# Hybrid decoder block on one core: the row norm of x from its natural layout, spread over the partitions by ones times a diagonal

## Chip, cores and metric

One core of one Trainium2 chip runs the whole program in a single launch. The metric is the device time of that launch in microseconds; lower is better.

## The reference, cut to what matters

The block starts with an RMS norm of `x` (1024 rows of 1024 values), and every projection reads its result:

```python
def rms_norm(x, w):
    xf = x.astype(jnp.float32)
    y = xf * lax.rsqrt(jnp.mean(xf * xf, axis=-1, keepdims=True) + EPS)
    return (y * w.astype(jnp.float32)).astype(x.dtype)

h = rms_norm(x, norm_w)
proj = h @ w_in          # split into the inputs of three mixers and the merge gates
...
x = x + merged @ w_out
```

After it come three mixers (a spatial gate, windowed attention, cross attention into `mem`), three projections under sigmoid gates, and an output projection with the residual add. The change touches only how the root mean square of each row of `x` is found and applied.

## The kernel before, in words

Every fp32 matmul of the large projections is made of three passes: each operand is split into a high part (a rounded cast by ScalarE, `A.copy`, L137) and a low part (the difference, by VectorE, L138), and `mm3` (L158) multiplies high by high, high by low and low by high. So weights and activations all pass through ScalarE and VectorE before TensorE uses them.

The host gives `x` twice: `xT`, transposed and cut into five column groups (columns are rows of x), and `x` in its natural layout (until now read only near the end, for the residual add). The groups are `x0` (rows 0 to 127), `x1` (rows 512 to 639), then `x2`, `x3`, `x4`, each of 256 columns: rows 128 a to 128 a + 127 and the same plus 512, for a = 1, 2, 3.

The prologue, L288 to L328, works through the groups. `load_x` (L231) starts the transfers of a group's pages from SyncE's queue (512 KB each, eight in all). `square_x` and `squares` (L237, L175) square a group on ScalarE into tiles of the ring `ws` (four buffers of 128x512 in `wpool`); for x3 and x4 VectorE first adds the tiles in pairs (L189). `sum_x` and `sum_squares` (L242, L193) multiply an all-ones matrix with the squares on TensorE, which sums over the partitions and leaves each column's sum in all 128 partitions of a PSUM bank (ring `tr`, two banks). `norm_x` and `normalize` (L245, L199) take the root on ScalarE (L203) and the reciprocal on VectorE (L204) over the whole 128 x width tile `rsx`, multiply `xT` by the norm weight and by `rsx` (VectorE, L208, eight instructions a group) and split the result. `sums` (L261) makes differences of normalized quarters for a fast matrix multiplication later. `proj_mq(j)` (L275) is the first projection: for each block of 128 rows j, in the order 0, 4, 1, 5, 2, 6, 3, 7, 24 matmuls of 128x512 with eight weight pieces `wq_[k]`. Blocks 0 and 4 need x0 and x1, blocks 1 and 5 need x2, 2 and 6 x3, 3 and 7 x4. The argument `between` puts a `sum_x` in the midst of a projection. After it come the `n` products (L968 on), whose first weights `wh_n`, `wl_n` are made while the projections end.

Three things set the order. The program is traced in the order of the lines, and a scheduler at compile time places each engine's instructions by that priority and by what it believes to be ready; at run time every engine's queue is in order. The eight pieces of `w_mq` (`raw`, L140) come through the same ring `ws` as the squares: a piece can only be transferred once the buffer's earlier user is done. And `rsx` lies in the ring `wl`, nine buffers, beside the weights' low parts.

Of the kernel before, what the change touches and what calls it, by code (L numbers as in the profile page):

```python
# [12 lines left out]
F32 = mybir.dt.float32  # L13
F32R = mybir.dt.float32r
I32 = mybir.dt.int32
AF = mybir.ActivationFunctionType
# [5 lines left out]
P = 128  # L22
D = 1024
# [18 lines left out]
def hybrid_block(  # L42
# [131 lines left out]

    def squares(xs, cw, name, eng, levels=1):  # L175

        kp = KT // len(xs)
        kq = 512 // cw
        sqs = []
        for k in range(0, KT, kq):  # L180
            sq = wpool.tile([P, kq, cw], F32, name=f"xq_{name}{k}", tag="ws", bufs=4)
            last[0] = A.activation(out=sq, in_=xs[k // kp][:, k % kp:k % kp + kq, :], func=AF.Square)
            sqs.append(sq)
        for _ in range(levels):
            h = len(sqs) // 2
            if h == 0:
                break
            for i in range(h):
                eng.tensor_tensor(out=sqs[i], in0=sqs[i], in1=sqs[h + i], op=ALU.add)  # L189
            sqs = sqs[:h]  # L190
        return [sq[:, k, :] for sq in sqs for k in range(kq)]

    def sum_squares(sqs, cw, name):  # L193
        pt = ps.tile([P, 512], F32, name=f"np_{name}", tag="tr")[:, :cw]
        for k, sq in enumerate(sqs):
            T.matmul(pt, lhsT=ones, rhs=sq, start=k == 0, stop=k == len(sqs) - 1)
        return pt

    def normalize(xs, pt, wcol, dst, cw, name, rs):  # L199


        kp = KT // len(xs)
        A.activation(out=rs, in_=pt, func=AF.Sqrt, scale=1.0 / D, bias=eps_c)  # L203
        V.reciprocal(out=rs, in_=rs)  # L204
        for k0 in range(0, KT, 4):
            xp, q = xs[k0 // kp], k0 % kp
            for k in range(4):
                V.scalar_tensor_tensor(out=xp[:, q + k, :], in0=xp[:, q + k, :], scalar=wcol[:, k0 + k:k0 + k + 1],  # L208
                                       in1=rs, op0=ALU.mult, op1=ALU.mult)
            for hi, lo, xv in dst(k0, xp[:, q:q + 4, :]):  # L210
                split(hi, lo, xv)
# [19 lines left out]
    def load_x(i):  # L231
        o = sum(widths[:i]) * KT
        xcs.append(load_cols(xT[:, o:o + widths[i] * KT], widths[i], f"x{i}"))

    sq_ = {}

    def square_x(i):  # L237
        sq_[i] = squares(xcs[i], widths[i], f"x{i}", V, int(i > 2))

    sm_ = {}  # L240

    def sum_x(i):  # L242
        sm_[i] = sum_squares(sq_[i], widths[i], f"x{i}")

    def norm_x(i):  # L245
        def dst(k0, xv):
# [7 lines left out]
            if k0 == 0:  # L254
# [3 lines left out]
                    + (xv.rearrange("p k (b t) -> p k b t", b=2),)]  # L258
        normalize(xcs[i], sm_[i], nw, dst, widths[i], f"x{i}", rs=rsx[:, 256 * (i % 2):256 * (i % 2) + widths[i]])

# [27 lines left out]
    rsx = wpool.tile([P, WW], F32, name="rsx", tag="wl", bufs=9)  # L288
    load_x(0)
    load_consts()  # L290
    wraw = [raw(w_mq[:, k * 512:(k + 1) * 512], 512, f"mq{k}") for k in range(2)]
    load_x(1)
    square_x(0)
    sum_x(0)
    with tc.issue_after(last[0].ins):
        wq_ = [parts(wraw[k], 512, f"mq{k}") for k in range(2)]
    norm_x(0)
    for k in range(2, 4):
        wq_.append(parts(raw(w_mq[:, k * 512:(k + 1) * 512], 512, f"mq{k}"), 512, f"mq{k}"))
    square_x(1)  # L300
    sum_x(1)
# [711 lines left out]
    with tc.tile_pool(name="ppool", reuse_waits="tile", bufs=1, side="right") as pp_:  # L1013
# [41 lines left out]
        def mem_norm(c):  # L1055
            cs = slice(c * P, (c + 1) * P)
            normalize([xm[c]], sm[c], mw,
                      lambda k0, xv: [(mem[0][:, k0:k0 + 4, cs], mem[1][:, k0:k0 + 4, cs], xv)], P, f"mem{c}", page([P, 256], f"rs_mem{c}", tag="th")[:, :P])

# [457 lines left out]
```

## Time and profile before

| | |
|---|---|
| median of 3 runs | 1120.58 us (1119.02 to 1123.42) |
| the profiled execution's own time | 1120.26 us |
| its span, first to last instruction | 1118.5 us |
| TensorE busy | 1092.7 us, 98% |
| VectorE busy | 794.1 us, 71% |
| ScalarE busy | 514.0 us, 46% |
| mean granted TensorE clock | 0.994 of full speed |

The profile is one execution. A busy share is a mean over the whole span: it says which engine carries the kernel, and the stretches of the prologue have to be looked at by themselves. The three runs differ by 0.4%.

### The profile page before, as it was taken

The numbers are of one execution on the slowest core, as the hardware profiler recorded it, in microseconds if no ns is written. First come the engines' busy times: TensorE is split into PE (matmuls) and PEld (weight loads), VectorE is DVE, ScalarE is ACT, GpSimd is POOL, SyncE is SP. The second block draws the span as 40 slices with busy tenths as digits, with TensorE's granted clock in tenths as the row PEclk, the third lists the DMA queues.
The fourth block names the chain that finished last, engine by engine and source line by source line (L and its number), as shares of the span: only waits on it lengthen the run. The fifth ranks groups of instructions, "written<-read, shape, count | busy, mean of one in ns | idle before, by whom it ended". The sixth has DMA issues, their size and how long they took to land.

```text
span 1118.5 us, 18302 instructions
## 1 busy us (share of the span) xinstructions
PE 1092.7 (98%) x6680; PEld 955.9 (85%) x6680; DVE 794.1 (71%) x1701; ACT 514.0 (46%) x1123; POOL 195.7 (17%) x250
## 2 busy tenths in 40 slices
PE   8989999999999999999999999999999999998998
PEld 7879999999988887888888888888888787886998
DVE  6999899856687766656555656687885467568863
ACT  6553333223245543755665554666564562134320
POOL 0000431321000002011111111111111026511232
PEclk9999999999999999999999999999999999999999
DMA  7222322454242423444434325455544975665432
GB/s 236 76 96 91 128 86 96 144 190 151 72 142 94 129 98 119 143 147 153 128 121 136 124 95 181 123 180 157 166 132 132 335 273 160 173 161 136 142 107 83
DMA packets 84558, 157.57 MB, mean 141 GB/s; under 512 B 9605, under 2 KB 30708, under 8 KB 84468
## 3 DMA queue, kind: packets, MB, share of 16 engines
q1 hardware_dynamic: 68164, 106.87, 30.6%
q0 software_dynamic: 14864, 47.05, 13.0%
q10 hardware_dynamic: 1440, 2.49, 0.6%
q8 instruction: 52, 0.85, 0.3%
q14 instruction: 38, 0.31, 0.1%
HBM read 106.84 MB, written 48.22 MB: 139 GB/s over the span
## 4 chain that ended last, share of the span: by engine, by line
PE 86%; DVE 5%; DMA 4%; issue 3%; POOL 1%; ACT 1%; SPq 0%; POOLq 0%; DVEq 0%; ACTq 0%
PE t L159 12%; PE t L161 12%; PE t L160 11%; PE n L160 7%; PE n L159 7%; PE n L161 7%; PE po L606 3%; PE pp L159 2%; DMA merged<-tg 2%; PE pp L161 2%; PE pp L160 2%; PE po L160 2%; PE po L159 2%; PE po L161 2%; PE pt L599 1%
## 5 line engine op out<-in xcount | busy, mean ns | idle before, releaser
L159 PE MATMUL t<-th,wh_t 128*128 128x512 f32 x336 | 135.2, 402 | 0.0
L161 PE MATMUL t<-th,wl_t 128*128 128x512 f32 x336 | 132.0, 393 | 0.0
L160 PE MATMUL t<-tl,wh_t 128*128 128x512 f32 x336 | 131.4, 391 | 0.0
L159 PE MATMUL n<-wh_n,th 128*128 128x256 f32 x384 | 108.2, 282 | 0.0
L161 PE MATMUL n<-wh_n,tl 128*128 128x256 f32 x384 | 107.6, 280 | 0.0
L160 PE MATMUL n<-wl_n,th 128*128 128x256 f32 x384 | 107.6, 280 | 0.0
L161 PEld LDWEIGHTS t<-th,wl_t 128*128 128x128 f32 x336 | 63.1, 188 | 14.5
L159 PEld LDWEIGHTS n<-wh_n,th 128*128 128x128 f32 x384 | 73.3, 191 | 1.5 <-issue 0.9
L160 PEld LDWEIGHTS t<-tl,wh_t 128*128 128x128 f32 x336 | 63.3, 188 | 12.8
L159 PEld LDWEIGHTS t<-th,wh_t 128*128 128x128 f32 x336 | 63.3, 188 | 12.3
L160 PEld LDWEIGHTS n<-wl_n,th 128*128 128x128 f32 x384 | 72.1, 188 | 0.2 <-issue 0.2
L161 PEld LDWEIGHTS n<-wh_n,tl 128*128 128x128 f32 x384 | 72.2, 188 | 0.0
L159 PE MATMUL t<-H2h,wh_t 128*128 128x512 f32 x168 | 67.8, 404 | 0.0
L137 ACT CAST wh_t<-ws_t 128x512 fp32r<-128x512 f32 x86 | 51.8, 619 | 33.3 <-PE n L161 11.8
L161 PE MATMUL t<-H2h,wl_t 128*128 128x512 f32 x168 | 65.9, 392 | 0.0
L160 PE MATMUL t<-H2l,wh_t 128*128 128x512 f32 x168 | 65.5, 390 | 0.0
L138 DVE TENSOR_TENSOR wl_t<-ws_t,wh_t 128x512 fp32r<-128x512 f32 x86 | 58.2, 685 | 10.0 <-ACT wh_t L137 9.9
L1069 DVE TENSOR_TENSOR o<-t,sa 128x512 f32<-128x512 f32 x63 | 43.3, 687 | 29.5 <-PE t L161 25.1
L1038 POOL DMA_DIRECT2D scr_g<-o x48 | 26.1, 544 | 191.9 <-ACT o L1024 167.1
L939 POOL TENSOR_TENSOR on<-on,nss 128x1024 f32<-128x1024 f32 x12 | 26.2, 2205 | 173.4 <-DVE nss L134 116.0
L159 PE MATMUL n<-wh_n,H2h 128*128 128x256 f32 x192 | 54.9, 286 | 0.1
L160 PE MATMUL n<-wl_n,H2h 128*128 128x256 f32 x192 | 54.3, 283 | 0.0
(382 smaller groups left out, 3185.1 us busy)
## 6 DMA issues: line engine op xcount, KB each, us to landing
ws_t<-in_w_t SPq DMA_DIRECT2D x64, 256.0 KB, 3.5
scr_g<-o POOLq DMA_DIRECT2D x48, 256.0 KB, 2.7
tg<-scr_g SPq DMA_DIRECT2D x16, 512.0 KB, 3.9
ws_n<-in_w_n SPq DMA_DIRECT2D x24, 256.0 KB, 3.3
wr_n<-in_w_n SPq DMA_DIRECT2D x24, 256.0 KB, 3.3
scr_qk<-on POOLq DMA_DIRECT2D x12, 512.0 KB, 4.3
bx<-scr_qk SPq DMA_DIRECT2D x24, 256.0 KB, 3.3
wr_t<-in_w_t SPq DMA_DIRECT2D x20, 256.0 KB, 3.5
```

The lines of the kernel that those rows point to most:

```text
L137: A.copy(out=hi, in_=y)
L138: (eng or V).tensor_tensor(out=lo, in0=y, in1=hi.bitcast(F32), op=ALU.subtract)
L159: T.matmul(o, lhsT=ah, rhs=bh, start=first, stop=False)
L160: T.matmul(o, lhsT=ah, rhs=bl, start=False, stop=False)
L161: T.matmul(o, lhsT=al, rhs=bh, start=False, stop=last)
L599: T.transpose(p2[:, h * P:(h + 1) * P], c.pr[h // 2][:, h % 2, b * P:(b + 1) * P], ident)
L606: T.matmul(po[:, 64 * h:64 * h + 64], lhsT=c.pT[b][:, h * P:(h + 1) * P], rhs=mb.v[:, (t - nk + 1 + b) % 3, 64 * h:64 * h + 64], start=b = ...
L939: G.tensor_tensor(out=v, in0=v, in1=ss[:, 16 * ORD[q]:16 * ORD[q] + 16].unsqueeze(2) .to_broadcast([P, 16, 64]), op=ALU.mult)
L1038: G.dma_start(out=t[:, h], in_=d)
L1069: V.tensor_tensor(out=o[q], in0=psum, in1=s, op=ALU.add)
```

## The change

The sums of squares of x are no longer made from `xT`. For each block t of 128 rows, `square_x` now loads the natural rows of `x` in two halves of 128x512 (16 transfers of 256 KB in all, from SyncE's queue, into the ring `ws`), and ScalarE squares each half with an accumulator output, which leaves the row sums in one column of `ssq`. VectorE adds the two halves, ScalarE takes the root and VectorE the reciprocal, each on a 128x1 column. `sum_x` then multiplies the identity by that column (VectorE, 128x128, into a quarter of `rsx`) and TensorE multiplies ones with that diagonal: 1/rms of the block's rows stands in all partitions of a PSUM bank. `normalize` reads it from PSUM as its second tensor operand. `square_x(0)` stands ahead of the constants and the first weights, and `square_x(1)` behind `norm_x(0)`, ahead of weight pieces 2 and 3. `square_x(2)`, `(3)`, `(4)` stay where they were. The norm of `mem` keeps its way: its root and reciprocal are written out in `mem_norm`.

```diff
-    def squares(xs, cw, name, eng, levels=1):
...
-            last[0] = A.activation(out=sq, in_=xs[k // kp][:, k % kp:k % kp + kq, :], func=AF.Square)
...
-                eng.tensor_tensor(out=sqs[i], in0=sqs[i], in1=sqs[h + i], op=ALU.add)
...
-    def normalize(xs, pt, wcol, dst, cw, name, rs):
+    def normalize(xs, rs, wcol, dst):
...
-        A.activation(out=rs, in_=pt, func=AF.Sqrt, scale=1.0 / D, bias=eps_c)
-        V.reciprocal(out=rs, in_=rs)
...
-    sq_ = {}
+    GROUPS = ((0,), (4,), (1, 5), (2, 6), (3, 7))
+    ssq = const.tile([P, 32], F32, name="ssq")
+    rst = const.tile([P, 16], F32, name="rst")
 
     def square_x(i):
-        sq_[i] = squares(xcs[i], widths[i], f"x{i}", V, int(i > 2))
+        for t in GROUPS[i]:
+            for h in range(2):
+                xn = wpool.tile([P, WW], F32, name=f"xn{t}{h}", tag="ws", bufs=4)
+                nc.sync.dma_start(out=xn, in_=x[t * P:(t + 1) * P, 512 * h:512 * h + 512])
+                last[0] = A.activation(out=xn, in_=xn, func=AF.Square, accum_out=ssq[:, 2 * t + h:2 * t + h + 1])
+            r = rst[:, 2 * t:2 * t + 1]
+            V.tensor_tensor(out=r, in0=ssq[:, 2 * t:2 * t + 1], in1=ssq[:, 2 * t + 1:2 * t + 2], op=ALU.add)
+            A.activation(out=r, in_=r, func=AF.Sqrt, scale=1.0 / D, bias=eps_c)
+            V.reciprocal(out=rst[:, 2 * t + 1:2 * t + 2], in_=r)
...
     def sum_x(i):
-        sm_[i] = sum_squares(sq_[i], widths[i], f"x{i}")
+        pt = ps.tile([P, 512], F32, name=f"rs_x{i}", tag="tr")
+        for n, t in enumerate(GROUPS[i]):
+            dg = rsx[:, (t % 4) * P:(t % 4 + 1) * P]
+            V.tensor_scalar(out=dg, in0=ident, scalar1=rst[:, 2 * t + 1:2 * t + 2], scalar2=None, op0=ALU.mult)
+            T.matmul(pt[:, n * P:(n + 1) * P], lhsT=ones, rhs=dg, start=True, stop=True)
+        sm_[i] = pt[:, :widths[i]]
...
     load_x(0)
+    square_x(0)
     load_consts()
     wraw = [raw(w_mq[:, k * 512:(k + 1) * 512], 512, f"mq{k}") for k in range(2)]
     load_x(1)
-    square_x(0)
     sum_x(0)
     with tc.issue_after(last[0].ins):
         wq_ = [parts(wraw[k], 512, f"mq{k}") for k in range(2)]
     norm_x(0)
+    square_x(1)
     for k in range(2, 4):
         wq_.append(parts(raw(w_mq[:, k * 512:(k + 1) * 512], 512, f"mq{k}"), 512, f"mq{k}"))
-    square_x(1)
     sum_x(1)
```

## Rows read from the trace of the kernel before

**Rows 1.** The page's part 1: busy time, share and instructions of each engine.

```profile
PE 1092.7 (98%) x6680; PEld 955.9 (85%) x6680; DVE 794.1 (71%) x1701; ACT 514.0 (46%) x1123; POOL 195.7 (17%) x250
```

**Rows 2.** Stretches of the prologue: length, busy time by engine, clock, DMA share, GB/s.

```profile
9.50:14.50 5.00, 2.05 (x16) 1.86 (x16) 4.04 (x11) 2.66 (x6) 0.00 (x0) 1.00 0.84 287
...
18.00:23.00 5.00, 4.82 (x21) 3.80 (x21) 4.70 (x13) 4.27 (x8) 0.00 (x0) 1.00 0.97 340
23.00:30.00 7.00, 7.00 (x32) 5.67 (x32) 7.00 (x13) 5.73 (x12) 0.00 (x0) 1.00 0.22 83
...
55.00:70.00 15.00, 12.71 (x55) 9.64 (x53) 15.00 (x28) 9.82 (x18) 0.00 (x0) 1.00 0.09 35
70.00:100.00 30.00, 28.98 (x240) 28.41 (x239) 26.80 (x46) 11.52 (x22) 0.00 (x0) 1.00 0.40 134
```

**Rows 3.** Timeline of TensorE: start, length, what, idle before and releaser.

```profile
10.65 2.05 PE L196 MATMUL np_x<-xq_x,ones 128*128 128x128 f32 x16 [1.21 <-ACT xq_x L182]
...
30.19 0.39 PE L159 MATMUL pq<-wh_mq,H1h 128*128 128x512 f32 x1
...
57.87 0.50 PE L159 MATMUL pq<-wh_mq,H1h 128*128 128x512 f32 x1 [2.01 <-ACT H1h L137]
...
69.65 0.40 PE L159 MATMUL n<-wh_n,H1h 128*128 128x256 f32 x2
```

**Rows 4.** Chain that ended last, prologue: start, length, what.

```profile
8.94 4.37 DMA ws_mq<-in_w_mq
...
19.74 3.68 PE np_x L196 x16
...
32.39 1.78 PE np_x L196 x8
...
46.99 1.73 PE np_x L196 x8
...
53.38 1.67 DVE rsx L204
...
72.61 0.61 DVE wl_n L138
```

**Rows 5.** Groups of VectorE by shape, first 75 us: busy, mean ns, idle before.

```profile
L208 DVE SCALAR_TENSOR_TENSOR xs_x<-xs_x,colt,rsx 128x256 f32<-128x256 f32 x24 | 9.8, 485 | 0.0
...
L204 DVE RECIPROCAL rsx<-rsx 128x256 f32<-128x256 f32 x3 | 5.3, 1752 | 0.0
L208 DVE SCALAR_TENSOR_TENSOR xs_x<-xs_x,colt,rsx 128x128 f32<-128x128 f32 x16 | 4.4, 347 | 0.0
...
L189 DVE TENSOR_TENSOR xq_x<-xq_x,xq_x 128x512 f32<-128x512 f32 x4 | 2.6, 699 | 0.0
...
L204 DVE RECIPROCAL rsx<-rsx 128x128 f32<-128x128 f32 x2 | 1.9, 950 | 0.0
```

**Rows 6.** Groups by shape, whole span: the nearest prices for the new operations.

```profile
L95 DVE TENSOR_SCALAR gb<-gb 128x24 f32<-128x24 f32 x1 | 0.2, 178 | 0.0
L733 DVE RECIPROCAL st_m<-st_m 128x2 f32<-128x2 f32 x16 | 2.6, 165 | 8.5 <-ACT pr_m L730 8.5
L911 DVE SCALAR_TENSOR_TENSOR off<-prs,colt,bsb 128x128 f32<-128x128 f32 x4 | 1.4, 347 | 0.0
L182 ACT ACTIVATE xq_x<-xs_x 128x512 f32<-128x512 f32 x16 | 9.3, 621 | 2.8 <-DMA xs_x<-in_xT 2.4 <-PE np_x L196 0.2
L591 ACT ACTIVATION_READ_ACCUMULATOR pr<-pr,ng 128x1 f32 x96 | 18.1, 188 | 0.0
L83 ACT ACTIVATE warm<-eps_c 128x1 f32<-128x1 f32 x1 | 0.2, 203 | 0.0
```

**Rows 7.** Transfers of the first 30 us: totals.

```profile
DMA packets 2786, 6.61 MB, mean 220 GB/s; under 512 B 608, under 2 KB 608, under 8 KB 2784
```

**Rows 8.** TensorE's clock around an idle stretch near the end (columns of rows 2).

```profile
1026.00:1028.00 2.00, 0.92 (x4) 0.95 (x5) 1.97 (x4) 0.63 (x1) 0.77 (x1) 0.73 0.39 106
1028.00:1030.00 2.00, 2.00 (x12) 2.00 (x11) 1.97 (x4) 0.32 (x1) 0.08 (x1) 0.50 0.90 180
```

More of the change, by code (lines that the diff above doesn't have):

```diff
@@ L173, in hybrid_block @@
     last = [None]
-    def squares(xs, cw, name, eng, levels=1):
[L177 to L181, printed above, removed]
-            last[0] = A.activation(out=sq, in_=xs[k // kp][:, k % kp:k % kp + kq, :], func=AF.Square)
[L183 to L188, printed above, removed]
-                eng.tensor_tensor(out=sqs[i], in0=sqs[i], in1=sqs[h + i], op=ALU.add)
-            sqs = sqs[:h]
-        return [sq[:, k, :] for sq in sqs for k in range(kq)]
     def sum_squares(sqs, cw, name):
@@ L258, in dst @@
                     + (xv.rearrange("p k (b t) -> p k b t", b=2),)]
-        normalize(xcs[i], sm_[i], nw, dst, widths[i], f"x{i}", rs=rsx[:, 256 * (i % 2):256 * (i % 2) + widths[i]])
+        normalize(xcs[i], sm_[i], nw, dst)
     def sums(a):
@@ L1056, in mem_norm @@
             cs = slice(c * P, (c + 1) * P)
-            normalize([xm[c]], sm[c], mw,
-                      lambda k0, xv: [(mem[0][:, k0:k0 + 4, cs], mem[1][:, k0:k0 + 4, cs], xv)], P, f"mem{c}", page([P, 256], f"rs_mem{c}", tag="th")[:, :P])
+            rs = page([P, 256], f"rs_mem{c}", tag="th")[:, :P]
+            A.activation(out=rs, in_=sm[c], func=AF.Sqrt, scale=1.0 / D, bias=eps_c)
+            V.reciprocal(out=rs, in_=rs)
+            normalize([xm[c]], rs, mw,
+                      lambda k0, xv: [(mem[0][:, k0:k0 + 4, cs], mem[1][:, k0:k0 + 4, cs], xv)])
         mem_steps = {6: [lambda: mem_squares(0)], 7: [lambda: mem_norm(0), lambda: mem_load(1)],
```

## The prediction

> **What bounds the kernel now.** I read the page's part 1 first: TensorE is busy 98% of the span [rows 1]. So only two things can shorten the run: less work on TensorE, or fewer waits of TensorE. The change touches the prologue alone, so I then cut its 100 us into stretches [rows 2] and laid TensorE's timeline [rows 3] and the chain that ended last [rows 4] beside them.
>
> The reader should see three regimes. Up to about 23 us the transfers set the pace: DMA share 0.84 to 0.97 at 287 to 340 GB/s, and the chain runs through the weight pieces, one of which holds it for 4.37 us [rows 2, 4]. From 23 us on VectorE is busy all the time, in 23 to 30 and again in 55 to 70, where it has 15.00 of 15.00 us while TensorE has 12.71 [rows 2]. In between TensorE's own work carries the chain, and the sums over the partitions stand in it with 3.68, 1.78 and 1.73 us [rows 4]. Block 1 of the projections, the first that needs x2, at 30.19; x4 makes TensorE wait 2.01 us at 57.87; the n products begin at 69.65 [rows 3], limp until the chain leaves VectorE at about 73 [rows 4], and TensorE lacks 1.0 us in 70 to 100 [rows 2]. After 100 us nothing of the change is left.
>
> **The change, part by part.** The sum is made against the profiled execution's own 1120.26 us, 0.3 below the median of 1120.58.
>
> *TensorE.* The sums of x2, x3, x4 leave the stream: 3.68 + 1.78 + 1.73 = 7.2 us [rows 4]. Six diagonal products take their place. An fp32 product of 128 columns costs 2.05 / 8 = 0.26 us (16 records are 8 products) [rows 3], so 1.5 us come in, and 5.7 go. The sums of x0 and x1 lie ahead of the stream, under the wait for weights.
>
> *VectorE.* Out go the wide reciprocals, 5.3 + 1.9 us, and the pair sums, 2.6 us: 9.8 us busy [rows 5]. In come, for each of eight blocks, a 128x1 add and a 128x1 reciprocal (165 ns for 128x2), and the identity times a column, 128x128. The page has no such row; below it is bounded by the 128x24 scalar operation, 178 ns, above by the 128x128 multiplication, 347 ns [rows 5, 6]. Its shape is that of the upper, its one tensor operand that of the lower; I take 0.25. With 0.16 for the add, 8 x 0.58 = 4.6 us (4.0 to 5.4), net 5 us less.
>
> The 40 multiplications of L208 now read 1/rms from PSUM. The row with a PSUM operand, L911, takes 347 ns at 128x128, exactly what L208 takes from SBUF [rows 5, 6], so I count nothing. [...]
>
> *ScalarE.* Sixteen squares stay; each gains an accumulator read of 188 ns, 3.0 us, and eight column roots of 0.20 replace five wide ones [rows 6]. ScalarE has 9.82 of 15 us to do in 55 to 70 and 5.73 of 7 in 23 to 30 [rows 2], so its throughput hides this; if that cover went, 2.5 us would show. What is not hidden is its order: squares now wait for their own transfers, and casts of weights stand behind them.
>
> *SyncE and the transfers.* This is the price. Sixteen transfers of 0.26 MB are added, 4.2 MB, and they pass through the ring `ws` with the weight pieces. Before, 6.61 MB moved in the first 30 us [rows 7], all but 0.6 of it by 23 us (7 us at 83 GB/s come after) [rows 2]. The natural tiles of x0, x1 and x2 are eight, 2.1 MB, and those of x2 are traced behind every page of x3 and x4, so they land last. At 287 to 340 GB/s 2.1 MB last 6.2 to 7.3 us: x2 is complete at about 30. If instead x3's and x4's pages (also 2.1 MB) let them pass, it is 23. The queue is in order of the program, hence nearer the upper end; I take 28.
>
> The weight pieces slip too: 0.52 MB of x0 go ahead of the first piece, about 1.8 us at 287 GB/s, and an in-order queue that stands at a natural tile without a free buffer holds all pieces behind it. Blocks 0 and 4 then end some 2 us later than they could. I cost that at nothing, because TensorE waits for x2 anyway; with x2 at 23 it would show.
>
> *From x2 to block 1.* After the last landing: square and accumulator 0.62 + 0.19, add 0.16, root 0.20, reciprocal 0.17, diagonal 0.25, product 0.26, four multiplications at 9.8 / 24 = 0.41 make 1.64, cast 0.62: 4.1 us, the cast taken at the price of the square of the same shape [rows 3, 5, 6]. So block 1 starts at 32.1 instead of 30.19: 1.9 us late.
>
> TensorE itself would be ready at 30.19 - 3.68 = 26.5 and idles some 5 us. What such a gap does to the clock shows near the end: after an idle stretch the granted clock reads 0.73 and 0.50 in two stretches of 2 us [rows 8], which is 2 x 0.27 + 2 x 0.50 = 1.5 us lost. The wait of 2.01 us at 57.87 left it at 1.00 [rows 2, 3]. I add 1.5.
>
> *From block 1 to the n products.* Before 69.65 - 30.19 = 39.46 us. Of it go the two sums, 1.78 + 1.73, and the wait of 2.01, since VectorE, with its 5 us less and with `sums(0)` drawn into the gap while x2 is awaited, has x4 ready in time. Four diagonals add 1.0. That leaves 34.9, with the clock 36.4: the n products start at 32.1 + 36.4 = 68.5, 1.15 early. VectorE's queue ends earlier as well, so the 1.0 us that TensorE lacks after 70 comes back: 2.15 in all, rounded to 2.2. **Forecast 1120.26 - 2.2 = 1118.1 us.**
>
> Nothing for the rest: `mem_norm` issues the same instructions; `rsx` frees its buffer of `wl` earlier; a PSUM bank of `tr` is held until the multiplications are done, but the next user of the bank is two groups on, behind those in the same queues.
>
> Written with the landing time L, the end moves by L - 30.2 as long as TensorE idles enough to lose its clock.
>
> **The rivals.**
>
> *Early landing: a full gain.* If x3's and x4's pages give way, L is 23, block 1 starts at 27.1, the gap stays under the one that kept its clock, and the end moves by (27.1 - 30.19) - 4.5 - 1.0 = -8.6: 1111.7. For it: DMA share is only 0.22 in 23 to 30 [rows 2]. Against it: the order of the program.
>
> *Late landing: slower.* The four tiles of x2 are the 13th to 16th users of a ring of four, behind two natural groups and eight pieces. A round is a landing of 4.37 [rows 4] and about 1.4 us of cast and difference, 0.62 and 0.70 by the rows of that shape [rows 5, 6]. The first buffer is free again at 8.94 [rows 4], so two more rounds and a landing end at 8.94 + 2 x 5.8 + 4.4 = 25. If the added pages and tiles double a landing to 8.7 us, a round is 10.1 and L is 8.94 + 20.2 + 8.7 = 37.8: 7.6 slower, 1127.9. It decides from L above 30.2, where the change stops paying, and from 36 it can be measured. For it: the transfers already fill 0.97 [rows 2]. Against it: 340 GB/s were reached just when the queue was deepest.
>
> *VectorE stays the bound.* If its order is not better filled, the 5.7 us of TensorE turn into waits like that at 57.87, and the end stays at about 1120.3. For it: 15.00 of 15.00 us busy [rows 2]. Against it: its own work shrinks by about the same 5 us.
>
> **How the numbers follow.** Half a per cent, 5.6 us, is about what a measurement of this kernel tells from no change. Forecast (L from 26 to 32) 0.54, VectorE as the bound 0.13: both within it, 0.67. Early landing 0.20, the part faster by more than 0.5%. Late landing 0.13, the part slower. The range reaches toward both rivals and leaves about one in ten out on either side: 1112.0 to 1124.5; it holds the page's 2.6 us for PSUM and the diagonal's bounds. The forecast's own range is 1116 to 1122.
>
> **What would show it.** Right: no L189 and no wide reciprocal; L208 still at about 347 and 485 ns; the projections' third block starts near 32, after TensorE idled for several us, with a stretch of halved clock; no long wait before x4; the n products start near 68.5 and do not limp; ScalarE waits longest for the natural tiles of x2. Wrong: x2's natural tiles landing before 25 or after 34, TensorE waiting at x3 or x4, or a difference that arises after 100 us.

## The result and the profile after

The changed kernel takes 1128.03 us (median of 6 runs, 1124.56 to 1130.36) against 1119.93 us for the kernel before on the same chips (6 runs): ratio 1.0066, 95% interval 1.0049 to 1.0083, slower by 7.4 us by the ratio; the medians lie 8.1 us apart. The profiled execution took 1129.19 us with a span of 1127.5. The forecast was 1118.1, the range ended at 1124.5.

The page's part 1 of the changed kernel, which answers to [rows 1]: TensorE has two microseconds more and VectorE four less, over a span that is 9 us longer.

```profile
PE 1094.6 (97%) x6632; PEld 954.0 (85%) x6632; DVE 789.8 (70%) x1716; ACT 516.3 (46%) x1142; POOL 195.9 (17%) x250
```

The stretches of the prologue, changed kernel (columns as in [rows 2]: busy time by engine, granted clock, DMA share, GB/s):

```profile
9.50:14.50 5.00, 1.81 (x4) 1.41 (x5) 4.67 (x14) 3.59 (x9) 0.00 (x0) 0.59 0.66 163
18.00:23.00 5.00, 4.12 (x16) 2.23 (x15) 4.91 (x13) 3.18 (x6) 0.00 (x0) 1.00 0.92 299
23.00:30.00 7.00, 5.28 (x22) 4.03 (x22) 5.68 (x10) 2.87 (x6) 0.00 (x0) 1.00 0.99 362
30.00:40.00 10.00, 1.59 (x4) 1.00 (x4) 4.29 (x13) 7.50 (x23) 0.00 (x0) 0.54 0.69 217
55.00:70.00 15.00, 15.00 (x69) 12.13 (x68) 13.93 (x26) 7.52 (x13) 0.00 (x0) 1.00 0.14 52
70.00:100.00 30.00, 29.05 (x214) 27.48 (x213) 27.76 (x47) 14.79 (x28) 0.00 (x0) 1.00 0.42 140
```

The reader should see three things. The transfers, quiet from 23 to 30 us before (0.22), are now full (0.99). Between 30 and 40 TensorE has 1.59 us of work and VectorE 4.29. And from 55 on the limit has changed hands: TensorE has 15.00 of 15.00 us, VectorE 13.93, where it was the other way round [rows 2].

Up to 23 us as many bytes have moved as before (6.00 MB, before 6.03); the slow stretch from 9.5 to 14.5 is made good by then. The natural tiles come behind: by 30 us it is 8.53 MB instead of 6.61 [rows 7]. SyncE's issues of x2's four tiles, changed kernel (start, length, what):

```profile
20.67 4.06 SPq L224 DMA_DIRECT2D xn<-in_x  x4
```

For three of them the trace tells how long they took from issue to landing (the tile `xn` in the window from 20 to 25 us):

```profile
DMA to landing us min/median/max: 8.5/9.6/9.8
```

They were issued at 20.67, 21.14 and 23.10 us and landed at about 30.3, 30.9 and 31.6. The fourth landed before its square began, by 32.83 at the latest (ScalarE's timeline below).

TensorE's timeline, changed kernel (start, length, what, and in brackets the idle time before with what ended it); it answers to [rows 3]:

```profile
12.69 0.80 PE L159 MATMUL pq<-wh_mq,H1h 128*128 128x512 f32 x1 [4.05 <-ACT H1h L137]
...
27.89 0.39 PE L161 MATMUL pq<-wh_mq,H2l 128*128 128x512 f32 x1
33.50 0.79 PE L239 MATMUL rs_x<-rsx,ones 128*128 128x128 f32 x2 [5.22 <-DVE rsx L238]
34.70 0.80 PE L239 MATMUL rs_x<-rsx,ones 128*128 128x128 f32 x2 [0.41 <-DVE rsx L238]
40.08 0.79 PE L159 MATMUL pq<-wh_mq,H1h 128*128 128x512 f32 x1 [4.59 <-ACT H1h L137]
...
76.40 0.28 PE L159 MATMUL n<-wh_n,H1h 128*128 128x256 f32 x1
```

Block 0 begins 1.8 us sooner than before, but block 1, the first that needs x2, begins at 40.08 instead of 30.19: 9.9 us late. After 28.3 us TensorE does nothing but the two diagonal products. The n products begin at 76.40 instead of 69.65, 6.75 us late. Then the lag does not come back, it grows: the first product of t starts at 322.95 (before 314.49, 8.5 us late), and the span ends 9.0 us late. So there are two places to explain, 28 to 40 us, and everything behind 76.

What stands between x2's landing and block 1 is in ScalarE's timeline, changed kernel:

```profile
22.72 0.34 ACTq L283 DMA_DIRECT2D scr_q<-qnat  x1
...
29.80 0.58 ACT L280 COPY qnat<-pq 128x512 f32<-128x512 f32 x1 [2.23 <-DMA scr_q<-qnat]
30.29 0.63 ACT L225 ACTIVATE xn<-xn 128x512 f32<-128x512 f32 x1
...
32.83 0.61 ACT L225 ACTIVATE xn<-xn 128x512 f32<-128x512 f32 x1
33.35 0.19 ACT L225 ACTIVATION_READ_ACCUMULATOR xn<-xn 128x1 f32 x1
...
36.71 0.63 ACT L225 ACTIVATE xn<-xn 128x512 f32<-128x512 f32 x1 [2.04 <-DMA xn<-in_x]
...
37.96 0.60 ACT L137 CAST th<-xs_x 128x512 fp32r<-128x512 f32 x1
38.80 0.63 ACT L225 ACTIVATE xn<-xn 128x512 f32<-128x512 f32 x1 [0.24 <-DMA xn<-in_x]
39.34 0.19 ACT L225 ACTIVATION_READ_ACCUMULATOR xn<-xn 128x1 f32 x1
39.43 0.60 ACT L137 CAST H1h<-xs_x 128x512 fp32r<-128x512 f32 x1
```

The copy ahead of x2's squares waits 2.23 us for the store of `scr_q` to free `qnat`, but x2's first tile lands only as that wait ends, so here it costs next to nothing. The squares follow the landings, and the last sum is read at 33.35. The cast H1h that block 1 waits for stands behind squares of x3, one of which waits 2.04 us for its own natural tile, and behind a cast of the `sums`. VectorE had begun x2's multiplications at 35.53. The clock of 0.59 between 9.5 and 14.5 us (the first blocks run after a wait of 4.05 us) is not in the loss: TensorE is done with all it has at 28.3 and waits.

The new operations, VectorE's groups by shape in the first 80 us of the changed kernel (busy, mean ns, idle before); they answer to [rows 5, 6]:

```profile
L188 DVE SCALAR_TENSOR_TENSOR xs_x<-xs_x,colt,rs_x 128x256 f32<-128x256 f32 x24 | 10.0, 476 | 0.9 <-PE rs_x L239 0.9
...
L188 DVE SCALAR_TENSOR_TENSOR xs_x<-xs_x,colt,rs_x 128x128 f32<-128x128 f32 x16 | 4.6, 341 | 1.1 <-PE rs_x L239 1.1
...
L238 DVE TENSOR_SCALAR rsx<-ident,rst 128x128 f32<-128x128 f32 x8 | 2.3, 284 | 2.5 <-PE rs_x L239 2.2
...
L227 DVE TENSOR_TENSOR rst<-ssq 128x1 f32<-128x1 f32 x8 | 1.2, 157 | 1.1 <-ACT xn L225 1.0
L229 DVE RECIPROCAL rst<-rst 128x1 f32<-128x1 f32 x8 | 1.1, 156 | 1.3 <-ACT rst L228 1.3
```

1/rms from PSUM costs the multiplications nothing: 341 and 476 ns, against 347 and 485 from SBUF. The prices of this part of the sum held.

### The profile page after: what moved, and what is told of

It reads as the page before. It is cut to its first block, busy times and chain, and to the rows that moved or that the text cites. A ratio compares the mean times of both kernels' runs of the same rounds, so it can differ in the third digit from the quotient of the medians.

```text
span 1127.5 us, 18270 instructions
## 1 busy us (share of the span) xinstructions
PE 1094.6 (97%) x6632; PEld 954.0 (85%) x6632; DVE 789.8 (70%) x1716; ACT 516.3 (46%) x1142; POOL 195.9 (17%) x250
## 3 DMA queue, kind: packets, MB, share of 16 engines
q1 hardware_dynamic: 70468, 111.06, 31.6%
## 5 line engine op out<-in xcount | busy, mean ns | idle before, releaser
L1069 DVE TENSOR_TENSOR o<-t,sa 128x512 f32<-128x512 f32 x63 | 43.3, 687 | 30.9 <-PE t L161 28.4
L161 PE MATMUL n<-wh_n,H2l 128*128 128x256 f32 x192 | 54.3, 283 | 0.0
```

The source lines that it names most:

```text
L161: T.matmul(o, lhsT=al, rhs=bh, start=False, stop=last)
L1069: V.tensor_tensor(out=o[q], in0=psum, in1=s, op=ALU.add)
```

## The experiments

Each run is compared with the kernel before on the same chip, in the same minutes (its median lay between 1120.17 and 1121.33 us in these sessions). Here are all timed ones, with two marks from their profiles: the start of the first n product and of the first t product. The marks are those of one profiled execution, whose own time stands beside them. That time can lie off the median: 5.9 us above it in e15, 3.4 in e10 and 2.0 in e9, 3.2 below it in e2 and 2.5 in e4.

| run | n starts | t starts | profiled, us | time, us | ratio to before (95%) |
|---|---|---|---|---|---|
| before (first profile; profile again) | 69.65; 70.55 | 314.49; 314.94 | 1120.26; 1118.58 | 1120 | 1 |
| the changed kernel | 76.40 | 322.95 | 1129.19 | 1128.03 | 1.0066 (1.0049 to 1.0083) |
| e1, x2 first | 70.19 | 318.15 | 1124.61 | 1124.11 | 1.0034 (1.0024 to 1.0045) |
| e2, cast first | 71.96 | 318.50 | 1122.32 | 1125.53 | 1.0036 (1.0019 to 1.0053) |
| e3, no late loads | 65.25 | 314.48 | 1123.36 | 1122.42 | 1.0008 (0.9992 to 1.0023) |
| e4, both | 70.12 | 318.06 | 1121.95 | 1124.43 | 1.0038 (1.0023 to 1.0052) |
| e5, x2 the old way | 67.12 | 316.36 | 1121.44 | 1120.18 | 0.9995 (0.9986 to 1.0005) |
| e6, x3 and x4 only | 67.63 | 314.41 | 1122.21 | 1121.52 | 1.0003 (0.9989 to 1.0018) |
| e7, kept warm | 74.49 | 319.82 | 1128.32 | 1128.00 | 1.0062 (1.0041 to 1.0083) |
| e8, before + 192 bytes | 70.67 | 317.61 | 1126.24 | 1125.44 | 1.0042 (1.0031 to 1.0054) |
| e9, changed, no tile moved | 75.54 | 320.04 | 1123.79 | 1121.81 | 1.0008 (0.9996 to 1.0019) |
| e17, the same again | 74.69 | 319.20 | 1122.53 | 1123.24 | 1.0028 (1.0013 to 1.0044) |
| e10, e5 with no tile moved | 67.17 | 314.64 | 1120.11 | 1116.70 | 0.9966 (0.9952 to 0.9980) |
| e11, e6 with no tile moved | 66.75 | 311.74 | 1119.30 | 1117.49 | 0.9974 (0.9961 to 0.9988) |
| e12, e1 with no tile moved | 72.37 | 317.51 | 1119.72 | 1120.83 | 0.9998 (0.9984 to 1.0012) |
| e13, before + 64 bytes | 70.98 | 319.23 | 1121.57 | 1122.30 | 1.0011 (0.9999 to 1.0022) |
| e14, before + 128 bytes | 68.63 | 311.97 | 1122.77 | 1122.63 | 1.0013 (1.0001 to 1.0026) |
| e15, before, H 64 bytes apart | 71.57 | 315.31 | 1121.65 | 1115.74 | 0.9949 (0.9930 to 0.9968) |
| e16, e10 and e15 together | 68.59 | 307.65 | 1112.58 | 1113.34 | 0.9937 (0.9913 to 0.9960) |

### First question: what makes block 1 late

**e1_x2_first** lets x2's natural tiles pass the pages of x3 and x4 on SyncE.

```diff
...
-                nc.sync.dma_start(out=xn, in_=x[t * P:(t + 1) * P, 512 * h:512 * h + 512])
+                lastdma[0] = nc.sync.dma_start(out=xn, in_=x[t * P:(t + 1) * P, 512 * h:512 * h + 512])
...
     load_x(2)
-    load_x(3)
-    load_x(4)
     norm_x(1)
     square_x(2)
+    with tc.issue_after(lastdma[0].ins):
+        load_x(3)
+        load_x(4)
```

> The transfers of x3's and x4's pages (2.1 MB) are put behind x2's four natural tiles on SyncE's queue; bytes and operations are the same. Theory A (queue order: x2's tiles wait behind the pages): block 1 of the projections starts near 31 us instead of 40.08, the gap before it shrinks from about 12 to 4 us or less, and the time falls by 6 to 8 us to about 1121. Rival B (the added 4.2 MB as such, wherever they stand): block 1 still starts after 37 and the time falls by less than 2 us.

Block 1 started at 34.70, its wait for H1h was still 5.64 us, and n started at 70.19, all but even with the kernel before. The time fell by 3.9 us, not by the whole loss, and t still came 3.7 us late. What held block 1 now was a store: x2's last tile landed at about 25.3, VectorE began x2's multiplications at 28.63, but H1h's cast stands in ScalarE's queue behind a copy that waits for the store of `scr_q`, issued at 26.34 and landed 6.6 us later. ScalarE in e1:

```profile
33.04 0.58 ACT L281 COPY qnat<-pq 128x512 f32<-128x512 f32 x1 [4.13 <-DMA scr_q<-qnat]
...
34.04 0.60 ACT L137 CAST H1h<-xs_x 128x512 fp32r<-128x512 f32 x1
```

**e2_cast_first** leaves the loads and puts the squares of x3 behind the last cast of x2.

```diff
...
-        A.copy(out=hi, in_=y)
+        lastcast[0] = A.copy(out=hi, in_=y)
...
-    square_x(3)
+    with tc.issue_after(lastcast[0].ins):
+        square_x(3)
```

> ScalarE does the squares of x3 and x4 only behind the casts of x2 (H1h, h12h, H2h); the transfers stay as in the changed kernel. Theory C (ScalarE's order: the cast H1h stands behind squares that wait for their transfers): the cast starts within 0.4 us of the fourth multiplication of x2, block 1 starts at about 37.8 instead of 40.08, and the time falls by 2 to 3 us. Theory A alone (only the landing of x2 counts): block 1 moves by under 0.5 us. A third outcome would be that block 1 starts earlier but x3 comes late, and the time stays within 1 us.

Block 1 started at 36.22 instead of 40.08, n at 71.96. The 3.9 us between the two are not ScalarE's order alone. In this execution x2's first three tiles landed at 28.3, 28.9 and 29.6, 2.0 us sooner than in the changed kernel's profile; block 0 had already started 1.0 us sooner (11.65 instead of 12.69), which the edit does not touch. From the last square of x2 to block 1 it took 5.07 us (31.15 to 36.22) instead of 7.25 (32.83 to 40.08): the order itself is worth 2.2 us, as the expectation had it.

**e3_no_loads** leaves out the natural loads of x2, x3 and x4; ScalarE squares pages of xT of the same size instead, so the sums of these blocks are of other numbers.

```diff
+                if i < 2:
+                    src = xn
                     nc.sync.dma_start(out=xn, in_=x[...])
+                else:
+                    src = xcs[i][t // 4][:, 2 * h:2 * h + 2, :].rearrange("p a b -> p (a b)")
-                last[0] = A.activation(out=xn, in_=xn, func=AF.Square, ...)
+                last[0] = A.activation(out=xn, in_=src, func=AF.Square, ...)
```

> The twelve natural tiles of x2, x3 and x4 are not loaded; ScalarE squares the pages of xT in their place, with the accumulator, so these groups are scaled with other numbers. All small operations, the diagonal products and the PSUM operand stay. If the transfers are the whole loss (A or B): block 1 starts at about 27, TensorE does not wait more than 2 us, and the time is 1112 to 1115, 5 to 8 below the kernel before. Rival D (the small operations and their hand-overs between engines cost what is saved): 1119 or more.

Without the loads block 1 starts at 30.52 and n at 65.25, 4.4 us sooner than before: the work that the change saves is real. But t starts at 314.48, where it starts before, and the whole is no faster.

**e4_both** has the edits of e1 and e2 together.

> The edits of the first two together. If queue order and ScalarE's order are separate losses, the gains add up while TensorE is still waiting: block 1 near 30.5, 1119 to 1121. If the landing is what counts, it equals the first run within 1 us.

Block 1 started at 33.63, n at 70.12, and the time is that of e1: with x2 first, the order of x3's squares counts for next to nothing, and ScalarE's copy again waits for the store, 3.81 us.

So the lateness of block 1 has three causes that overlap, all in queues: the place of x2's tiles at the end of SyncE's, the squares of x3 ahead of the cast in ScalarE's, and, once x2 lands sooner, ScalarE's wait for a store that lands late among the added transfers (this one is read from the traces; no run moves the store). None of them explains why all four variants lose 2 to 5 us between n and t, where nothing of the change is left.

### Second question: what is lost behind the n products

**b_again** profiles the kernel before once more, beside the others.

> The kernel before, unchanged, profiled beside the runs that follow. All four runs so far lost 2 to 4 us between the start of the n products and 318 us against the first profile of the kernel before. If that loss belongs to the changed kernels, this profile reaches t at 314.5 us again, as the first did (within 0.5 us). If it belongs to the execution (another chip, another start of the instruction stream), t comes at 316 to 318 us here too, and only what lies before the n products needs a cause.

t at 314.94, the span 1116.9: the loss belongs to the changed kernels, not to a chip.

**e5_old_x2** and **e6_late_pair** keep the new sums only where their loads are no burden: all but x2, or x3 and x4 alone.

```diff
+    NATURAL = (0, 1, 3, 4)      # e6: (3, 4)
     def square_x(i):
+        if i not in NATURAL:
+            sq_[i] = squares(xcs[i], widths[i], f"x{i}", V, int(i > 2))
+            return
...
     def sum_x(i):
+        if i not in NATURAL:
+            sm_[i] = sum_squares(sq_[i], widths[i], f"x{i}")
+            return
...
```

> The changed kernel, but x2 alone gets its sums the old way (squares of its transposed pages by ScalarE, sixteen products with ones), so that nothing of x2 waits for natural tiles at the end of SyncE's queue. Theory (x2's natural tiles land too late, and everything else in the change is sound): block 1 starts at 30 us or before, TensorE does 2 to 4 us less than the kernel before ahead of the n products, which start at 65 to 68 us, and the whole takes 1116 to 1118 us. Rival (the products of x3 and x4 or VectorE's order are at fault as well): block 1 starts at 30 us, but the whole stays at 1120 to 1124 us.

> The kernel before, with only x3 and x4 summed in the new way; the start, x0 to x2, is as before. VectorE loses its adds of squares (9.8 us, all of x3 and x4) and gets about 2.5 us of diagonals, adds and reciprocals; SyncE gets 2.1 MB more, after the dense stretch. Theory (the early loads were the fault, the saving is real): VectorE ends its sums 4 to 7 us sooner, n starts at 65 to 68 us, the whole takes 1115 to 1118 us. Rival (VectorE's saving is not on the path): 1119.5 to 1121 us.

In both TensorE is busy without a break from 30 to 40, and n starts 2 to 2.5 us sooner than in the first profile of the kernel before. Both times are those of the kernel before all the same. (e6 also has the statements at the start in the old order.) The theory that only the late landing was at fault falls here.

**e7_keep_warm** fills the gap of the changed kernel with 36 spare products.

```diff
...
+    warmth = ps.tile([P, 512], F32, name="warmth", tag="sc")
+    for m in (lastmm[0], lastdg[2]):
+        with tc.issue_after(m.ins):
+            for _ in range(18):
+                T.matmul(warmth[:, :P], lhsT=ones, rhs=ones, start=True, stop=True)
```

> The changed kernel with 36 spare products of ones by ones (128x128) in the gap in which TensorE waits for x2: 18 ahead of its diagonals, 18 behind them; the result is not touched. Theory (part of the loss is the clock, that falls to 0.50 in the gap and is paid by the two diagonals and by the first 11 products of block 1 at 0.43 instead of 0.23 us): the granted clock stays at 1.00 through the gap, block 1 starts 0.5 us sooner and runs at 0.23 us from its first product, n starts 2 to 3 us sooner, the whole takes 1125 to 1126.5 us. Rival (VectorE, not TensorE, sets the start of the n products by then): n and the whole move by less than 0.7 us, 1127.5 to 1128.5 us.

The stretch from 30 to 40 us in e7 (columns as in the stretches above):

```profile
30.00:40.00 10.00, 7.42 (x56) 6.41 (x55) 5.73 (x16) 7.80 (x25) 0.00 (x0) 1.00 0.65 220
```

The granted clock is 1.00 where the changed kernel has 0.54 (0.50 in each 2 us from 32 to 44). Block 1 starts at 38.97 and n 1.9 us sooner, but 1.15 us of that was there at block 0 (11.54 instead of 12.69), ahead of the spare products; from block 1 to n it took 35.52 us instead of 36.32, so the clock is worth about 0.8 us there. The median does not move (1128.00), though with four runs a gain of that size would not show. The clock of the gap is not what the 7.4 us hang on.

In TensorE's timeline every variant showed products of n that start some 119 ns apart over the whole stage, while those of both profiles before fall to 113.5 in places. The order of TensorE's instructions there is the same but for a few places. What differs is the addresses (they come from the allocation of each kernel; the traces hold none): the change adds two small constant tiles, 192 bytes a partition, and all that is allocated behind them from the low end (the pieces wh and wl, H1, H2) moves up by as much; th and tl, allocated from the high end, stay.

**e8_pad_only** is the kernel before with nothing but an unused tile of 192 bytes.

```diff
     mss = const.tile([P, 32], F32, name="mss")
+    pad = const.tile([P, 48], F32, name="pad")
+    V.memset(pad, 0.0)
```

> The kernel before with one unused tile of 192 bytes per partition among its constants, as many as the change's two small tiles take; nothing else. What is allocated behind it from the low end (the weight pieces, H1 and H2) moves up by 192 bytes, what is allocated from the high end (th, tl) does not. Theory of the placement (the n products run at 119 instead of 118 ns a product, and at 119 instead of 113.5 ns around 250 us, because the operands lie elsewhere): n starts with the kernel before (69.7 to 70.6 us), t comes 2 to 3 us later than before, as in all changed kernels, and the whole takes 1122 to 1124 us. Rival (the placement is nothing to TensorE; the pitch follows from what the other engines do meanwhile): the pitch of the first profile, 1119.5 to 1121.5 us.

The ratio is 1.0042: 4.7 us for an unused tile, more than the theory asked for. Between n and t it takes 246.9 us, where the two profiles of the kernel before take 244.8 and 244.4. The one instruction that fills the tile is not the cause: the runs e13 to e15 below have one too, and one of them is faster than the kernel before.

**e9_same_places**, **e10_old_x2_places**, **e11_late_pair_places** and **e12_x2_first_places** are the changed kernel, e5, e6 and e1, each with its sums in columns of the constant tile `avs`, which is used only much later. In each pair all that is allocated from the low end lies 192 bytes apart and nothing else differs. Against the kernel before every tile keeps its place, but for some buffers of the rings that e9, e10 and e12 take in another order, whole multiples of 2048 bytes away.

```diff
-    ssq = const.tile([P, 32], F32, name="ssq")
-    rst = const.tile([P, 16], F32, name="rst")
+    avs = const.tile([P, 2 * KT], F32, name="avs")
...
-                last[0] = A.activation(..., accum_out=ssq[:, 2 * t + h:2 * t + h + 1])
-            r = rst[:, 2 * t:2 * t + 1]
+                last[0] = A.activation(..., accum_out=avs[:, 2 * t + h:2 * t + h + 1])
+            r = avs[:, 2 * t:2 * t + 1]
...
```

> The changed kernel with its sums of squares and roots in columns of a constant tile that is there already and used only much later, so that no tile moves against the kernel before. Theory of the placement: the n products run as in the kernel before, the late landing of x2 stays: n starts at 76 us, the whole takes 1125 to 1126.5 us. Rival: 1127 to 1129 us, as the changed kernel.

> The kernel with x2 alone summed the old way, and no tile moved. Theory of the placement: n starts at 67 us as with the tiles moved, and keeps most of it: t 2 us sooner than with the tiles moved, the whole takes 1117 to 1118.5 us. Rival: 1120 us, as with the tiles moved.

> The kernel before with x3 and x4 alone summed the new way, and no tile moved. Theory of the placement: n starts at 67.5 us and t comes 2 us sooner than with the tiles moved; the whole takes 1117.5 to 1119 us. Rival: 1120.5 to 1121.5 us, as with the tiles moved.

> The changed kernel with both faults taken out: x2's natural tiles ahead of the pages of x3 and x4 on SyncE, and no tile moved. With the tiles moved this order took 1124 us. Theory (two causes that add: the moved tiles some 5 us, the late x2 some 2 to 4 us): n starts at 70 us and t comes within 1.5 us of the kernel before; the whole takes 1118 to 1120 us. Rival (with the tiles in place the late x2 costs nothing any more, since the changed kernel with the tiles in place takes 1121.8 us for other reasons, ScalarE's and VectorE's order): 1121 to 1122.5 us.

Five pairs now differ in the place of the tiles alone, and all five differ by the same sign and about the same size. Only the first pair ran side by side; the others come from different sessions, so the last column takes the difference of their ratios to the kernel before:

| pair | tiles moved | in place | difference, us | difference of the ratios |
|---|---|---|---|---|
| kernel before (e8) | 1125.44 | 1120.17 | 5.3 | 0.42% |
| changed kernel (e9; e17) | 1128.03 | 1121.81; 1123.24 | 6.2; 4.8 | 0.58%; 0.38% |
| x2 the old way (e5, e10) | 1120.18 | 1116.70 | 3.5 | 0.29% |
| x3 and x4 only (e6, e11) | 1121.52 | 1117.49 | 4.0 | 0.29% |
| x2 first (e1, e12) | 1124.11 | 1120.83 | 3.3 | 0.36% |

In the profiles 1.7 to 2.9 us of each pair lie between n and t; where the rest lies was not taken apart.

**e17_same_places_again** repeats e9, whose time and profile did not agree.

> The changed kernel with no tile moved, once more, since its time (1121.8 us, ratio 1.0008) and its profile (t 5.6 us late, and no sooner than the slowest of its ten runs) do not agree on what the late landing of x2 costs alone. Theory (two causes that add): 1123 to 1125 us against 1120 to 1121.5 us of the kernel before, ratio 1.002 to 1.004. Rival (the late landing is nearly all given back by the end): ratio 0.9995 to 1.0015 again, and a profile in which the lag of 5 to 6 us at t shrinks by 3 us or more by the end.

1.0028, as the theory had it; e9's interval reaches up to 1.0019 and this one down to 1.0013, so the two do not contradict each other. Not all of a longer stage between n and t is the place, though: e10 takes 247.5 us there with no tile moved, since n starts sooner than its weights are there (TensorE waits 1.70 us at 70.82). With the tiles in place the rest of the change costs 1 to 3 us, and with x2 first (e12) nothing that can be measured.

### Third question: what about the place

**e13_pad_64** and **e14_pad_128** are e8 with 16 and 32 columns instead of 48. **e15_h_apart** is the kernel before with 64 unused bytes ahead of H1 and H2 alone.

```diff
+    hpad = hpool.tile([P, 16], F32, name="hpad")
+    V.memset(hpad, 0.0)
     h11 = [hpool.tile([P, 4, 512], F32R, name=f"H1{c}") for c in "hl"]
```

> The kernel before with an unused constant tile of 64 bytes per partition. In the kernel before the stationary th and tl lie 64 bytes off the moving weight pieces, counted modulo 128 bytes, and H1, H2 lie at 0; in the changed kernel and in the kernel with 192 bytes more all lie at 0. The products against th run at 117.1 ns in the kernel before and at 118.9 in the one with 192 bytes more, those against H1 and H2 at 120 in both. Theory A (only the distance of the two operands modulo 128 bytes counts, 0 is slow): with 64 bytes all lie at 0 again: t comes 2.5 to 3 us late, 1124 to 1126 us. Rival B (the loss grows with the bytes moved, or any move away from the old places costs): 1121 to 1123 us, or a pitch that is neither of the two.

> The kernel before with an unused constant tile of 128 bytes per partition: everything from the low end moves, but the distance of th and tl from the weight pieces stays at 64 modulo 128 bytes. Theory A (only that distance counts): the pitch and the time of the kernel before, 1119.5 to 1121 us. Rival B (any move costs): 1122 to 1126 us.

> The kernel before with an unused tile of 64 bytes per partition ahead of H1 and H2 alone: they come to lie 64 bytes off the weight pieces modulo 128, as th and tl do already; nothing else moves. Theory A: the 864 n products against H1 and H2 fall from 120 to about 117 ns, 2 us or more less by t, and the products of the first stage and of t may gain as well: 1116 to 1118 us. Rival B: no change, 1119.5 to 1121 us, or a loss as with the other pads.

The rows to read are those of one tile's instructions, n, between 76 and 314 us: count, then the length of one in ns as min/median/max. The length holds a part that does not differ, some 163 ns in both stretches below; what differs is the distance to the next start. Two stretches of the timeline give the scale. In e13, of TensorE:

```profile
254.79 0.28 PE L161 MATMUL n<-wh_n,tl 128*128 128x256 f32 x1
...
257.90 0.28 PE L160 MATMUL n<-wl_n,th 128*128 128x256 f32 x1
```

26 products in 3.11 us, 119.6 ns each. In e16 (below), of TensorE:

```profile
254.78 0.28 PE L163 MATMUL n<-wh_n,tl 128*128 128x256 f32 x1
...
257.84 0.28 PE L163 MATMUL n<-wh_n,tl 128*128 128x256 f32 x1
```

27 products in 3.06 us, 113.3 ns each. In the rows of the tile n that is 283 against 276 ns. The kernel before, where th lies 64 bytes and H 0 bytes from the weight pieces (addresses as allocated, modulo 512):

```profile
L159 PE MATMUL n<-wh_n,th x384: 276/281/682, 83.0 to 307.5; 128*128 128x256 f32 x192
...
L160 PE MATMUL n<-wl_n,H2h x191: 278/283/283, 77.5 to 313.9; 128*128 128x256 f32 x191
```

e13: th at 0, H at 0.

```profile
L159 PE MATMUL n<-wh_n,th x384: 280/283/682, 84.4 to 312.3; 128*128 128x256 f32 x192
...
L160 PE MATMUL n<-wl_n,H2h x178: 277/283/283, 78.9 to 314.0; 128*128 128x256 f32 x178
```

e14: th at -64, H at 0.

```profile
L159 PE MATMUL n<-wh_n,th x384: 276/276/682, 82.0 to 305.0; 128*128 128x256 f32 x192
...
L160 PE MATMUL n<-wl_n,H2h x192: 278/283/287, 76.5 to 311.7; 128*128 128x256 f32 x192
```

e15: both at 64. The execution that these rows come from took 1121.65 us, 5.9 more than the median, so they do not show what the gain of the median is made of.

```profile
L161 PE MATMUL n<-wh_n,th x384: 278/281/682, 84.7 to 308.4; 128*128 128x256 f32 x192
...
L162 PE MATMUL n<-wl_n,H2h x188: 281/281/281, 79.2 to 313.7; 128*128 128x256 f32 x188
```

And the changed kernel, th at -128, H at 0:

```profile
L159 PE MATMUL n<-wh_n,th x378: 279/281/684, 89.4 to 313.8; 128*128 128x256 f32 x189
...
L159 PE MATMUL n<-wh_n,H2h x176: 278/283/385, 78.1 to 292.3; 128*128 128x256 f32 x176
```

Wherever the stationary operand lies at distance 0 from the moving one, the median is 283 (120.0 ns from start to start over the stage); at 64 to either side it is 281 or 276 (118 or 113 ns); at -128 it lies between (means of 118.6 to 119.2 over th and tl, where both profiles before have 116.3 to 117.2). For the n products the place decides between 120.0 and less: H left 283 only where it was moved against the pieces, and th came to 283 only where it came to 0. That -128 is not quite 0 speaks against counting modulo 128, as theory A did; whether 512 is the right count was not tested.

The whole did not follow so simply: e13 was expected at 1124 to 1126 and took 1122.3, e14 at 1119.5 to 1121 and took 1122.6. The products of t say part of why. There th and H are the moving side and the weight pieces the stationary one. The tile t from 330 to 860 us in the kernel before:

```profile
L161 PE MATMUL t<-th,wl_t x311: 388/392/481, 330.0 to 859.3; 128*128 128x512 f32 x156
```

In e13:

```profile
L161 PE MATMUL t<-th,wl_t x314: 388/389/478, 329.9 to 859.8; 128*128 128x512 f32 x157
```

In e14:

```profile
L161 PE MATMUL t<-th,wl_t x307: 390/394/482, 339.3 to 859.9; 128*128 128x512 f32 x154
```

In t the distance 0 is the quick one, by 3 to 5 ns in some 1000 products against th. So e13 lost 4.3 us up to t and had 2 of them back by 640 us, and e14 won 3.0 us up to t and had given them back by 850. Not all of that is the products' pace: near 706 us TensorE stands for 1.76 us in e14 and 1.82 in e13, ahead of a product on `mx`; in the first profile before it is 0.62 us and in the second under 0.25. The product waits there for ScalarE. The changed kernel's 192 bytes are bad in both stages. What the place does to the stages behind t was not taken apart.

**e16_old_x2_h_apart** puts the two gains together: e10 with H set 64 bytes apart.

> Candidate to beat both: x2 alone summed the old way, no tile moved, and H1 and H2 set 64 bytes off the weight pieces. Theory (the two gains add: 3.5 us from the new sums where they land in time, 4 to 5 us from the place of H1 and H2): 1111 to 1114 us. Rival (both gain the same microseconds ahead of t): 1115 to 1117 us.

1113.34 us, 6.9 less than the kernel before and the fastest of all: ratio 0.9937. That the gains of 3.5 and 5.6 us add in full, 9.1, is not excluded: the interval reaches from 4.5 to 9.7 us. Its n products all run at the quickest of the three lengths:

```profile
L161 PE MATMUL n<-wh_n,th x384: 275/276/682, 84.1 to 301.0; 128*128 128x256 f32 x192
...
L162 PE MATMUL n<-wl_n,H2h x192: 276/276/283, 78.9 to 307.4; 128*128 128x256 f32 x192
```

Why distance 64 gives 281 in e15 and 276 here is open, and the place alone does not settle it. In e10 th and the weight pieces lie at exactly the addresses that they have in e16, and its products against th come 117.1 ns apart on average, here 113.4; the kernel before shows both paces within one execution, each for many microseconds. The profiles of e10 and e15 come from executions 3.4 and 5.9 us above their medians; whether others run like e16 no profile shows.

## Why the prediction was wrong

**The step that failed most is one that was not in the sum: "After 100 us nothing of the change is left."** The change adds 192 bytes of constants, and the operands of TensorE move against each other. That costs 3.3 to 6.2 us (five pairs; for this kernel 4.8 and 6.2), the larger part of the 7.4. In the n and t stages part of it shows in products that carry no line of the diff; my last sentence named "a difference that arises after 100 us" as what would make it wrong, and it arose.

**The second step that failed is "So block 1 starts at 32.1".** Block 1 started at 40.08, 8.0 us later, and n, taken at 68.5, was 7.9 us wrong: that error arose here whole. Two of its terms were too small. The landing of x2 I took at 28, with bounds of 23 and 30; three tiles landed at 30.3, 30.9 and 31.6 and the last by 32.83, so 3.6 to 4.8 us of the error are there. The sum of bytes was right: 6.00 MB had moved by 23 us, and with x2's tiles the transfers are full until 30, the upper bound; I took 28, below it, and the last tile landed 1.6 to 2.8 us past it. From x2's last square to block 1 7.25 us went by, where I counted 4.1 for a bare chain without a queue, under the words "its throughput hides this"; I named ScalarE's order as not hidden and then gave it no price. The squares of x3 ahead of H1h's cast are 2.2 us of it, by e2.

**What held.** From block 1 to n I counted 36.4 us and it took 36.32, in part by luck: with the clock at 1.00 it took 35.52 in e7, where I counted 34.9, and the clock cost less than I added. The operations' prices held: PSUM costs the multiplications nothing, as row L911 said, and the rows show 0.2 us less at 128x256 (24 times 9 ns). The 2.6 us for PSUM that the range holds are shown by no run: the rows of the changed kernel read 341 and 476 ns from PSUM, against 347 and 485 from SBUF before. The diagonal was taken at 0.25 and took 0.284, the add at 0.16 and took 0.157. No L189, no wide reciprocal, and the wait before x4 gone: 15.00 of 15.00 us for TensorE from 55 to 70. The change does save time where its loads are no burden, as e3 (n 4.4 us sooner) and e10 (3.5 us) show.

**The clock.** I added 1.5 us; the granted clock was 0.54 in 30 to 40 and block 1's first 11 products started 0.43 us apart instead of 0.23, 2.2 us. But e7, with the clock back at 1.00, was only about 0.8 us quicker from block 1 to n, since other waits stand behind these products, and nothing of it can be seen at the end.

**The rivals.** The late landing, 1127.9, met the time by accident: its L of 37.8 did not occur. With the tiles in place the changed kernel was 0.9 and 3.1 us slower (e9, e17), inside the half per cent. "Early landing" was the direction of e1: x2 first took 3.9 us off with the tiles moved and 1 to 2.4 in place, not the 8.6 that I priced; x2 had landed at about 25, and block 1 then stood behind ScalarE's wait for the store. "VectorE stays the bound" did not come: VectorE had 13.93 of 15 us.

What stays open: how much of the late x2 is given back by the end (n is 4 to 6 us late in e9 and e17, the whole 1 to 3), where behind t the other part of the place's cost arises, and what beside the distance of the operands chooses between the two quicker paces.

## What to carry to other kernels

A change that allocates anything, be it a tile of 64 bytes (e13), moves what lies behind it; before a few microseconds are given to its mechanism, time the old kernel with the allocation alone, and the new one without it. Where a stage is bound by TensorE, look at the start-to-start distance of its products in both traces, and at the start addresses of the stationary and moving operands against each other. Before a profile is used to explain a median, look whether the profiled execution took about that long. And for work put on an engine with time to spare, price the instruction that will stand behind it in the queue, not the engine's share.

## What the hardware showed that I had not expected

Within one execution of the kernel before, at a granted clock of 1.00 from 76 to 314 us, the same product takes 113.5, 118 or 120.0 ns from start to start. With the stationary and the moving operand at the same place in SBUF, counted modulo 512 bytes (a count that was not tested), it takes 120.0 (283 in the rows) in every profile whose rows stand above; at 64 bytes to either side it takes one of the two shorter times (118 in e15, 113.3 in e16), and which one is not explained. Over the 2016 products of the stage 120.0 against 113.3 is an estimated 13 us; the stage took 248.2 us in e13, where both th and H lie at 0, and 239.1 in e16. The quickest long stretch read here, 143 products in e16, runs at 113.3. So e8, e13, e14 and e15 show that TensorE's own pace changes with the place of its two operands; by what mechanism no run shows.

A store of 0.26 MB on ScalarE's queue (`scr_q`) that lands in 2.0 to 2.2 us in the first 70 us of the kernel before took up to 7.0 us in the changed kernel: issued at 22.72, it was under way while the DMA share stood at 0.99 (23 to 30 us, before 0.22). With x2 first (e1) it took up to 6.6 us; without the late loads (e3) ScalarE has no wait for it in the first 80 us. The tile `scr_q` in the first 70 us of the changed kernel, from issue to landing as min/median/max:

```profile
DMA to landing us min/median/max: 2.0/3.2/7.0
```
